# Decay parameters and page table: contiguous broadcast rows and on-chip rearrangement in place of element-wise software loads

## The chip, the cores and the metric

The kernel runs on one core of one Trainium2 chip. The time is what the device takes for one execution, in microseconds (us); lower is better. A core has TensorE (PE; PEld is its weight load), VectorE (DVE), ScalarE (ACT), GpSimd (POOL) and SyncE (SP), each with its own instructions in a fixed order, and 16 DMA engines that move data between the chip's main memory and the on-chip memory of 128 partitions. A DMA that SyncE issues goes to the hardware queue q1, one that GpSimd issues to the software queue q0.

## What is computed

One inference step of a single decoder layer, in float32: 256 prompt tokens and 8 x 4 decoding tokens, model width 4096. The change touches the parameters of two of the three mixers, the gates of the delta rule and the paged cache.

```python
m = silu(c) @ w_ada + b_ada                          # modulation: shift, scale, gate
h = rmsnorm(x, g_norm) * (1 + scale) + shift
u_a, v_a, ..., a_b, b_b, q_c, k_c, ... = split(h @ w_in)      # one input projection
# delta rule: 16 heads, per-head decay
g = -exp(dn_a_log) * softplus(a_b + dn_dt_bias)      # dn_a_log, dn_dt_bias: 16 numbers each
beta = sigmoid(b_b)
o_b, s_new = gated_delta(q, k, v, g, beta, s0)
# sparse attention of the decoding tokens: page_table (8, 16) names the pages of the cache
kidx_past = cache_kidx[page_table]
idx = top_k(score(q_idx, kidx_past), 256)
k_sel, v_sel = cache_k[page_table[idx // 128], idx % 128], cache_v[...]
x = x + gate * (concat(y_a, y_b, y_c) @ w_out)
```

## The kernel before

A weaver writes the whole program at build time. Its main stream is a list of units: a `Gemm` unit multiplies one k-tile of 128 rows of w_in or w_out with the 288 tokens, an `Ada` unit makes modulation columns from w_ada. Every float32 weight tile `w` that is loaded (512 KB, two k-tiles, 4 buffers) is split into a high part `wh` by ScalarE and a low part `wl` by VectorE (4 buffers each), and TensorE adds three products into `acc`: wh with hH, wh with hL, wl with hH. The tiles `wa` and `ada` are weights and results of the modulation. Between the steps of this stream the weaver sets stages of side chains (Python generators), at places that it picks with its own rough clocks of the engines; `yield [tile]` goes on when the clock says that the tile is there. The order of each engine's instructions is fixed by this. SyncE issues all weight loads, one after the other, each once a buffer is free.

Phase 1 makes the modulation and runs the first columns of w_in group by group over 11 steps of feature tiles (`STEPS`; `lb` is its list of units by step). Phase 2 is opened by `phase2_open`: it frees the pools of phase 1 and starts the chains `small_gen` (indexer keys, decay, key and value rows), `idx_sample_gen` (indices of the pages, indexer of the decoding tokens), `sample_gen` and `prompt_gen` (attention), beside the rest of w_in; the delta rule, the gated MLP and the output projection follow.

At the third step from the end of phase 1 a chain with two parts is started:

```python
lb[-3][0].pre.append(lambda: W.push(lane(load_pages(), load_decay())))
```

`load_pages` reads the page table by 25 GpSimd loads into three tiles of int32: `ptp` (one entry for each partition), `pt2` (two entries) and `ptv` (eight entries), each in the layout that the index arithmetic of `idx_sample_gen` wants. `load_decay` fills the tiles `nega` (from dn_a_log) and `dtb` (from dn_dt_bias), 128 partitions x 36 columns: columns 0 to 31 hold the 16 heads twice, side by side (head, chunk), the same for all partitions, and columns 32 to 35 hold, for the 32 partitions of each of 4 groups, every fourth head. Each is written by two loads of 128 x 16 numbers whose neighbours lie two columns apart, and four loads of 32 x 4 numbers read four numbers apart. In `small_gen`, `nega` is first used by `A.activation(nega, nega, AF.Exp)`; in `idx_sample_gen`, the page tiles are used by the casts into `ptf` and `ptvf`, and the index tiles `ix8`, `ixk`, `ixv` feed the indirect gathers of `kraw` and `vraw`.

Every instruction goes through one recording helper, so the profile gives line 71 for all; tiles tell them apart.

Of the kernel before, what the change touches and what calls it, by code (L numbers as in the profile page):

```python
# [60 lines left out]
class Eng:  # L61
    """An engine whose instructions are noted by the weaver as they are emitted."""
# [15 lines left out]
class Gen:  # L78
    """A chain of stages that is emitted between the steps of the main stream.

    A stage that yields a function goes on when the function says so; one that yields tiles, when they are there.
    """
# [5 lines left out]
class Weaver:  # L88
    """Emits the main stream (weight loads, splits, matrix products) with the chains in between.

    The instructions are emitted in an order that suits the in-order engines: rough clocks of the engines tell when
    the operands of a chain's next stage are there.
    """
# [13 lines left out]
    # ---- clocks  # L107
# [18 lines left out]
    @staticmethod  # L126
    def span(ap):
        """The part of a tile that is used: the first to the last free element, and the partitions."""
        row = math.prod(list(ap.tensor.shape)[1:])
        dims = [(st, n) for st, n in ap.ap if n > 1]  # L130
        lo, p, n = ap.offset % row, ap.offset // row, 1
        if dims and dims[0][0] == row:
            n = dims.pop(0)[1]
        hi = lo + 1 + sum((k - 1) * abs(st) for st, k in dims)
        return (lo, hi, p, p + n) if hi <= row else (0, 1 << 40, 0, 1 << 40)

    def tile(self, pool, shape, dt, tag, name, bufs):
        """A tile; it can be written when its place's last tile is not used any more."""
# [68 lines left out]
    # ---- chains  # L207
# [37 lines left out]
    def finish(self, gens, until=None):  # L245
        """Emits the rest of the given chains, and of others where they wait for them."""
# [16 lines left out]
    def slot(self, name, n):  # L263
        """A chain goes on here when fewer than n others hold the named slot."""
# [4 lines left out]
    def lane(self, n=1):  # L269
        """A chain goes on here when its next n DMAs can start at once: each waits for the 8th before it."""  # L270
        yield lambda: all(self.lanes[(self.n_dma + i) % 8] <= self.t["T"] + 0.5 for i in range(n))

    def calm(self):
        """A chain goes on here with a large DMA when the weight loads leave the DMA queues some room."""
# [9 lines left out]
    def bank(self, n=1):  # L284
        """A chain goes on here when n banks are free."""
# [16 lines left out]
    # ---- main stream  # L302
    def prefetch(self, cur):
        """Loads and splits for the units after cur, as far as the buffers go."""
# [70 lines left out]
def tile_hybrid_step(ctx: ExitStack, tc: tile.TileContext, I, O):  # L375
# [39 lines left out]
    # ---------------------------------------------------------------- constants  # L415
# [4 lines left out]
    # 9 columns per k-tile; a quadrant takes 32, whose other rows go unused  # L420
# [15 lines left out]
    # ---------------------------------------------------------------- main stream  # L436
# [21 lines left out]
    class Gemm(Unit):  # L458
        """A k-tile of a group of up to 4 column tiles; two k-tiles are loaded together."""
# [38 lines left out]
    def group(w_ap, segs, tiles, kbs, finish, XH=hH, XL=hL):  # L498
# [5 lines left out]
        # the last two k-tiles go together, so that the tiles end one by one  # L504
# [5 lines left out]
    class Ada(Unit):  # L510
        """Modulation columns: the quadrants of the array take a quarter of a k-tile's columns each,

        or, of two k-tiles, half the columns of one each.
        """
# [46 lines left out]
    def ada_fin1(st, k0, n):  # L561
        """Shift and scale of n feature tiles, then their modulated tokens."""
# [40 lines left out]
    # ---------------------------------------------------------------- pools and loads of the first phase  # L603
# [14 lines left out]
    # the normed tokens lie where the low parts of the modulated ones go  # L618
# [8 lines left out]
    def load_x(i):  # L627
        src, n, _ = xsrc[i]
        if i == 2:
            # a quarter of a row on a partition  # L630
# [25 lines left out]

    ptp, pt2, ptv = (const([P, n], f"pt{n}", I32) for n in (1, 2, NB))
    pt = I["page_table"]

    def load_pages():  # L660
        G.dma_start(ptp, pt.rearrange("b (j o) -> (b j) o", o=1))
        for b in range(4):
            for u in range(2):
                p0 = 32 * b + 16 * u
                G.dma_start(pt2[p0:p0 + 16], bass.AP(tensor=pt.tensor, offset=pt.offset + 16 * b, ap=[[1, 16], [64, 2]]))
            yield from W.pause(4)
        for j in range(16):
            G.dma_start(ptv[8 * j:8 * j + 8], bass.AP(tensor=pt.tensor, offset=pt.offset + j, ap=[[0, 8], [16, NB]]))
            yield from W.pause(2)
# [129 lines left out]
    # ---------------------------------------------------------------- phase 1: modulation and the first columns  # L799
    def y_copy(f):  # L800
        """Frees the place of the low parts while half a tile's tokens are still to be modulated."""
# [96 lines left out]
    # the modulation of a step's feature tiles runs ahead of the products with them  # L898
# [13 lines left out]
    # spread so that the loads are as even as the steps allow  # L912
# [16 lines left out]
    # ---------------------------------------------------------------- phase 2  # L929
# [41 lines left out]
    def load_decay():  # L971
        for t, src in ((sc_["nega"], I["dn_a_log"]), (sc_["dtb"], I["dn_dt_bias"])):
            tpv = t[:, 0:32].rearrange("p (h c) -> p h c", c=2)
            for c in range(2):
                G.dma_start(tpv[:, :, c], bass.AP(tensor=src.tensor, offset=src.offset, ap=[[0, P], [1, 16]]))
            for hl in range(4):
                G.dma_start(t[32 * hl:32 * hl + 32, 32:36],
                            bass.AP(tensor=src.tensor, offset=src.offset + hl, ap=[[0, 32], [4, 4]]))
                yield from W.pause(2)

    def small_gen():
        sm = VT["c", 0]
        X.ki2 = tl("pa", [P, NTOK], "ki2")
# [23 lines left out]
        for t, o in ((av, 80), (bv, 96)):  # L1007
            tpv = t[:, 0:32].rearrange("p (h c) -> p h c", c=2)
            for c in range(2):
                V.tensor_copy(tpv[:, :, c], smt[:, c, o:o + 16])  # L1010
        yield [abD]
        for t, o in ((av, 80), (bv, 96)):
            dma2(t[:, 32:36], abD[0 if o == 80 else 1].rearrange("(g l) t -> (l t) g", l=4))
        # key and value rows, token-major
# [72 lines left out]
    # ---------------------------------------------------------------- attention  # L1087
# [99 lines left out]
    def idx_sample_gen():  # L1187
        # gather indices: 16-row pieces of the indexer pages, 4-row pieces of the key and value pages
# [6 lines left out]
        # 16 where the second half of the partition's 32 is  # L1195
# [13 lines left out]
        yield [ptp, pt2, ptv]  # L1209
        V.tensor_reduce(sub16, sv, axis=AX.X, op=OP.max)  # L1210
        ptf = tl("ap", [P, 3], "ptf")
        V.tensor_copy(ptf[:, 0:1], ptp)
        V.tensor_copy(ptf[:, 1:3], pt2)
# [6 lines left out]
        # row (page, eighth of the page, step) of the value pages, for partition (page, eighth)  # L1220
        ptvf = tl("ap", [P, NB], "ptvf")
        V.tensor_copy(ptvf, ptv)
# [45 lines left out]
        # scores: partition (quarter of the pages, token), column (page of the quarter, key of the page)  # L1268
# [78 lines left out]
    def topk_gen():  # L1347
        """The 256 best keys of every token: the best of the 4 segments in order, the lists merged, ties by position."""
        SC = X.SC
        # sums over the segments of a token, and over the segments before  # L1350
# [3 lines left out]
        for a in range(2):  # L1354
            for dq in range(-3, 4) if a == 0 else range(-3, 0):
                # partition p = 32 q' + r' counts for column 32 q + r where q' = q + dq and r' = r
# [1102 lines left out]
```

## Time and profile before

| | |
|---|---|
| three runs | 2720.19, 2716.18, 2720.14 us; median 2720.14 |
| the profiled execution: span from first to last instruction | 2716.4 us (no other time of this execution is recorded) |
| TensorE busy | 2553.7 us, 94% of the span |
| VectorE, ScalarE, GpSimd busy | 1622.0 (60%), 1062.6 (39%), 511.4 us (19%) |
| DMA | 616.09 MB, 227 GB/s in the mean |

Busy shares are means over stages with different limits. A stage is read by which wait ends last in it; the time of an engine that waits for nothing in a stage and is always busy is that stage's bound.

### The profile page before, as it was taken

What the parts mean: (1) busy time and instruction counts of PE and PEld (TensorE: products, weight loads), DVE (VectorE), ACT (ScalarE), POOL (GpSimd) and SP (SyncE); (2) the same over time, 40 slices, a digit from 0 to 9 for tenths busy, and PEclk for the clock granted to TensorE, in tenths of its full rate; (3) what the DMA queues carried; (4) which work ended last, traced back from release to release, by engine and by line L of the source; (5) the groups of instructions that cost most, each with busy time, mean ns of one, the idle gap of its engine ahead of it and who ended that gap; (6) DMA issues with size and microseconds to landing.
All of it is one profiled execution on the core that took longest, in us unless ns stands there. A gap on an engine that the chain in (4) does not pass through costs nothing.

```text
span 2716.4 us, 55357 instructions
## 1 busy us (share of the span) xinstructions
PE 2553.7 (94%) x21190; PEld 2275.1 (84%) x21190; DVE 1622.0 (60%) x3595; ACT 1062.6 (39%) x2440; POOL 511.4 (19%) x1169
## 2 busy tenths in 40 slices
PE   6999999992699999999999999999999999999997
PEld 3788888882579788878889988989989999999997
DVE  3477655551357778854457567667666567555554
ACT  4433222220224544334344444444444444444443
POOL 2000000201000123054453333442431210000000
PEclk9999999996799999999999999999999999999998
DMA  9999998898865657677777576567567466455554
GB/s 293 346 323 333 333 308 304 289 318 41 202 224 179 187 192 263 224 247 255 263 233 226 177 229 213 185 202 256 172 209 252 155 185 213 157 185 175 176 182 167
DMA packets 376849, 616.09 MB, mean 227 GB/s; under 512 B 49784, under 2 KB 150252, under 8 KB 376584
## 3 DMA queue, kind: packets, MB, share of 16 engines
q1 hardware_dynamic: 364296, 574.58, 64.3%
q0 software_dynamic: 12288, 37.97, 6.6%
q8 instruction: 167, 2.74, 0.4%
q14 instruction: 98, 0.80, 0.1%
HBM read 587.50 MB, written 24.95 MB: 225 GB/s over the span
## 4 chain that ended last, share of the span: by engine, by line
PE 83%; DMA 6%; another core or an unknown queue 3%; DVE 3%; issue 2%; POOL 2%; ACT 1%; SPq 0%; ACTq 0%; POOLq 0%; DVEq 0%
PE acc L71 65%; PE ada L71 7%; DMA w<-in_w_in_dram 2%; DMA wa<-in_w_ada_dram 1%; DMA vraw<-in_cache_v_dram,ixv 1%; PE Sup L71 1%; PE kT L71 1%; DVE wl L71 1%; PE YP L71 1%; PE v L71 1%; POOL vraw L71 1%; PE gram L71 1%; PE o L71 1%; PE S L71 1%
## 5 line engine op out<-in xcount | busy, mean ns | idle before, releaser
L71 DVE TENSOR_TENSOR wl<-w,wh 128x512 fp32r<-128x512 f32 (+1 forms) x1216 | 807.2, 682 | 810.0 <-ACT wh L71 783.4
L71 PE MATMUL acc<-hH,wh 128*128 128x288 f32 (+1 forms) x3744 | 1179.6, 315 | 58.8 <-ACT wh L71 47.6
L71 ACT CAST wh<-w 128x512 fp32r<-128x512 f32 (+1 forms) x1216 | 717.8, 611 | 1307.7 <-PE acc L71 916.4
L71 PE MATMUL acc<-hL,wh 128*128 128x288 f32 (+1 forms) x3744 | 1108.6, 296 | 0.4 <-DVE hL L71 0.4
L71 PE MATMUL acc<-hH,wl 128*128 128x288 f32 (+1 forms) x3744 | 1107.0, 296 | 0.4 <-DVE wl L71 0.4
L71 PEld LDWEIGHTS acc<-hH,wh 128*128 128x128 f32 (+1 forms) x3744 | 706.7, 189 | 201.2 <-ACT wh L71 92.6
L71 PEld LDWEIGHTS acc<-hL,wh 128*128 128x128 f32 (+1 forms) x3744 | 708.3, 189 | 7.9 <-issue 6.7
L71 PEld LDWEIGHTS acc<-hH,wl 128*128 128x128 f32 (+1 forms) x3744 | 707.4, 189 | 1.9 <-DVE wl L71 1.9
L71 PE MATMUL acc<-mL,wh 128*128 128x288 f32 x1024 | 302.7, 296 | 3.3 <-DVE mL L71 3.3
L71 PE MATMUL acc<-mH,wh 128*128 128x288 f32 x1024 | 304.4, 297 | 0.0
L71 PE MATMUL acc<-mH,wl 128*128 128x288 f32 x1024 | 302.9, 296 | 0.0
L71 PE MATMUL ada<-wa,cT 128*32 128x256 f32 x2048 | 159.2, 395 | 46.0 <-DMA wa<-in_w_ada_dram 44.9
L71 PEld LDWEIGHTS acc<-mL,wh 128*128 128x128 f32 x1024 | 193.1, 189 | 3.6 <-DVE mL L71 3.6
L71 PEld LDWEIGHTS acc<-mH,wl 128*128 128x128 f32 x1024 | 193.2, 189 | 0.0
L71 PEld LDWEIGHTS acc<-mH,wh 128*128 128x128 f32 x1024 | 193.0, 188 | 0.2
L71 PEld LDWEIGHTS ada<-wa,cT 128*32 128x32 f32 x2048 | 50.4, 110 | 97.0 <-DMA wa<-in_w_ada_dram 45.9
L71 DVE TENSOR_TENSOR zb<-zb,acc 128x288 f32<-128x288 f32 x160 | 70.6, 452 | 45.4 <-PE acc L71 44.4
L71 POOL TENSOR_TENSOR htmp<-yT,gaT 128x32 f32<-128x32 f32 x20 | 7.7, 386 | 474.6 <-DVE gaT L71 474.6
L71 POOL TENSOR_SCALAR frs<-frs 128x1 f32<-128x1 f32 (+1 forms) x3 | 0.9, 297 | 453.5 <-DVE frs L71 453.4
L71 PE MATMUL ada<-w,cT 128*32 128x256 f32 x1024 | 82.2, 391 | 0.0
L71 DVE TENSOR_TENSOR R<-R,R 128x248 f32<-128x248 f32 (+30 forms) x248 | 72.4, 292 | 6.9 <-DMA R<-dD 0.6
L71 POOL TENSOR_SCALAR tap<-xp,cwT 128x32 f32<-128x32 f32 x144 | 74.2, 515 | 0.4
(452 smaller groups left out, 2401.1 us busy)
## 6 DMA issues: line engine op xcount, KB each, us to landing
w<-in_w_in_dram SPq DMA_DIRECT2D x464, 512.0 KB
wa<-in_w_ada_dram SPq DMA_DIRECT2D x160, 512.0 KB
w<-in_w_ada_dram SPq DMA_DIRECT2D x128, 512.0 KB
w<-in_w_out_dram SPq DMA_DIRECT2D x128, 512.0 KB
wa<-in_w_ada_dram SPq DMA_DIRECT2D x192, 256.0 KB
St<-in_state_dn_dram SPq DMA_DIRECT2D x16, 512.0 KB
out_dram<-St SPq DMA_DIRECT2D x16, 512.0 KB
X<-in_x_prompt_dram SPq DMA_DIRECT2D x8, 512.0 KB
```

The costliest lines, as they stand in the source:

```text
L71: r = f(*a, **k)
```

## The change

The two parameter vectors are read in `small_gen`, at the opening of phase 2, as one row of 16 numbers (64 bytes) for each of the 128 partitions, by two loads on SyncE into `hp`. Twelve small VectorE copies put them where `nega` and `dtb` want them. The page table is read in `idx_sample_gen` as one row of all 128 entries (512 bytes) for each partition, by one load on SyncE into `pts`; VectorE casts it, multiplies it with masks (`ident`, `ptm`, `ptj`, which GpSimd makes) and sums along the row, so that each partition keeps its own entries. `load_pages`, `load_decay`, their pauses and the line that starts them are gone. The rest of the diff drops comments and is left out here.

```diff
-    ptp, pt2, ptv = (const([P, n], f"pt{n}", I32) for n in (1, 2, NB))
-    def load_pages():
-        G.dma_start(ptp, pt.rearrange("b (j o) -> (b j) o", o=1))
-        for b in range(4):
-            for u in range(2):
-                p0 = 32 * b + 16 * u
-                G.dma_start(pt2[p0:p0 + 16], bass.AP(tensor=pt.tensor, offset=pt.offset + 16 * b, ap=[[1, 16], [64, 2]]))
-            yield from W.pause(4)
-        for j in range(16):
-            G.dma_start(ptv[8 * j:8 * j + 8], bass.AP(tensor=pt.tensor, offset=pt.offset + j, ap=[[0, 8], [16, NB]]))
-            yield from W.pause(2)
...
-    def load_decay():
-        for t, src in ((sc_["nega"], I["dn_a_log"]), (sc_["dtb"], I["dn_dt_bias"])):
-            tpv = t[:, 0:32].rearrange("p (h c) -> p h c", c=2)
-            for c in range(2):
-                G.dma_start(tpv[:, :, c], bass.AP(tensor=src.tensor, offset=src.offset, ap=[[0, P], [1, 16]]))
-            for hl in range(4):
-                G.dma_start(t[32 * hl:32 * hl + 32, 32:36],
-                            bass.AP(tensor=src.tensor, offset=src.offset + hl, ap=[[0, 32], [4, 4]]))
-                yield from W.pause(2)
-
     def small_gen():
         sm = VT["c", 0]
+        hp = tl("pa", [P, 2, 16], "hp")
+        for i, src in enumerate((I["dn_a_log"], I["dn_dt_bias"])):
+            dma(hp[:, i], bass.AP(tensor=src.tensor, offset=src.offset, ap=[[0, P], [1, 16]]))
...
+        yield [hp]
+        for i, t in enumerate((nega, dtb)):
+            tpv = t[:, 0:32].rearrange("p (h c) -> p h c", c=2)
+            for c in range(2):
+                V.tensor_copy(tpv[:, :, c], hp[:, i])
+            for hl in range(4):
+                q = slice(32 * hl, 32 * hl + 32)
+                V.tensor_copy(t[q, 32:36], hp[q, i].rearrange("p (g l) -> p l g", l=4)[:, hl])
         yield [abD]
...
     def idx_sample_gen():
+        pts = tl("ap", [P, SEG], "pts", 1, tag="M")
+        pt = I["page_table"]
+        ptB, ptF, ptT = pts[:, 0:P].bitcast(I32), pts[:, P:2 * P], pts[:, 2 * P:3 * P]
+        dma(ptB, bass.AP(tensor=pt.tensor, offset=pt.offset, ap=[[0, P], [1, P]]))
...
-        yield [ptp, pt2, ptv]
+        ptm = pts[:, 384:448].rearrange("p (b j) -> p b j", j=16)
+        G.memset(ptm, 0.0)
+        for u in range(2):
+            G.affine_select(ptm, ptm, pattern=[[-32, 4], [-1, 16]], compare_op=OP.not_equal, fill=1.0,
+                            base=-16 * u, channel_multiplier=1)
+        ptj = pts[:, 448:464]
+        G.affine_select(ptj, ones[:, 0:16], pattern=[[-8, 16]], compare_op=OP.is_ge, fill=0.0, base=0,
+                        channel_multiplier=1)
+        G.affine_select(ptj, ptj, pattern=[[8, 16]], compare_op=OP.is_ge, fill=0.0, base=7, channel_multiplier=-1)
+        yield [ptB]
         V.tensor_reduce(sub16, sv, axis=AX.X, op=OP.max)
         ptf = tl("ap", [P, 3], "ptf")
-        V.tensor_copy(ptf[:, 0:1], ptp)
-        V.tensor_copy(ptf[:, 1:3], pt2)
+        ptvf = tl("ap", [P, NB], "ptvf")
+        V.tensor_copy(ptF, ptB)
+        V.tensor_tensor(ptT, ptF, ident, op=OP.mult)
+        V.tensor_reduce(ptf[:, 0:1], ptT, axis=AX.X, op=OP.add)
+        V.tensor_tensor(ptT.rearrange("p (h n) -> p h n", h=2), ptF.rearrange("p (h n) -> p h n", h=2),
+                        pts[:, 384:448][:, None].to_broadcast([P, 2, 64]), op=OP.mult)
+        V.tensor_reduce(ptf[:, 1:3], ptT.rearrange("p (h n) -> p h n", h=2), axis=AX.X, op=OP.add)
+        V.tensor_tensor(ptT.rearrange("p (b j) -> p b j", j=16), ptF.rearrange("p (b j) -> p b j", j=16),
+                        ptj[:, None].to_broadcast([P, NB, 16]), op=OP.mult)
+        V.tensor_reduce(ptvf, ptT.rearrange("p (b j) -> p b j", j=16), axis=AX.X, op=OP.add)
...
-        ptvf = tl("ap", [P, NB], "ptvf")
-        V.tensor_copy(ptvf, ptv)
...
-    lb[-3][0].pre.append(lambda: W.push(lane(load_pages(), load_decay())))
```

The instructions move at three places. On GpSimd, in the third step from the end of phase 1, these rows stand between the modulation of the feature tiles (`htmp`), and the 25 page-table loads stand likewise one step of feature tiles earlier; a row gives operation, output and input, the shape of the output side (partitions, then elements), and a count. Before:

```order
L71 TENSOR_TENSOR htmp<-htmp,shT 128x4x8
L71 DMA nega<-in_dn_a_log_dram 128x16x1 x2
L71 DMA nega<-in_dn_a_log_dram 32x4x1 x4
L71 DMA dtb<-in_dn_dt_bias_dram 128x16x1 x2
L71 DMA dtb<-in_dn_dt_bias_dram 32x4x1 x4
L71 TENSOR_TENSOR htmp<-yT_102,gaT 128x4x8
```

Now these rows and those of the page table are gone and the `htmp` rows follow each other; the last dimension of 1 in their shapes is a piece of one number.

On SyncE, at the opening of phase 2, behind the stores of the gate columns (`zD`). Before:

```order
L71 DMA zD_178<-zb_1263 128x288
L71 DMA w<-in_w_in_dram 128x2x512
L71 DMA wiD<-smt 32x16
L71 DMA abD<-v_c_571 32x32
L71 DMA out_dram<-smt 128x64 x2
```

Now:

```order
L71 DMA zD_175<-zb_1260 128x288
L71 DMA hp<-in_dn_a_log_dram 128x16
L71 DMA hp<-in_dn_dt_bias_dram 128x16
L71 DMA pts<-in_page_table_dram 128x128
L71 DMA w<-in_w_in_dram 128x2x512
L71 DMA wiD<-smt 32x16
L71 DMA abD<-v_c_568 32x32
```

The three new loads stand ahead of the first weight load behind the stores; all rows of SyncE ahead of this place are as before.

On VectorE at the same place, behind the index constants (`iop`); `pt` are the page tiles, `smt` and `wq` the transposed small columns, `wl` the splits of the main stream. Before:

```order
L71 TENSOR_SCALAR ptvf<-ptvf,iop 128x8
L71 TENSOR_TENSOR ixv<-ptvf,iof 128x64
L71 COPY smt<-smt 128x224
L71 COPY smt<-smt 32x112
L71 TENSOR_SCALAR wq<-smt 128x32
L71 TENSOR_TENSOR wl<-w,wh 128x512 x3
```

Now:

```order
L71 TENSOR_SCALAR iop<-iop 128x1
L71 COPY smt<-smt 128x224
L71 COPY smt<-smt 32x112
L71 TENSOR_SCALAR wq<-smt 128x32
L71 TENSOR_TENSOR wl<-w,wh 128x512 x2
L71 COPY av<-smt 128x16 x2
L71 COPY bv<-smt 128x16 x2
L71 COPY nega<-hp 128x16 x2
L71 COPY nega<-hp 32x4 x4
L71 COPY dtb<-hp 128x16 x2
L71 COPY dtb<-hp 32x4 x4
```

Before, the index arithmetic (it ends with `ixv`) stood ahead of `smt` and of all these splits. Now two `wl` splits come first, then the copies from `hp`, then the arithmetic on `pts` and the index arithmetic, and behind it the third and fourth split. TensorE's rows are the same up to the opening of phase 2; behind it the same products stand in a slightly other order.

## Rows read from the trace of the kernel before

**Rows 1.** The profile's page: the span, and the span in 40 equal slices of 67.9 us (PE: busy tenths of TensorE; GB/s: what the DMA engines moved).

```profile
span 2716.4 us, 55357 instructions
...
PE   6999999992699999999999999999999999999997
...
GB/s 293 346 323 333 333 308 304 289 318 41 202 224 179 187 192 263 224 247 255 263 233 226 177 229 213 185 202 256 172 209 252 155 185 213 157 185 175 176 182 167
```

**Rows 2.** Busy time by stage, core 0: the stretch in us from the span's start, its length, then busy time and instructions of PE, PEld, DVE, ACT and POOL, the granted clock of TensorE (1.00 is 2.4 GHz), the busy share of the 16 DMA engines, and GB/s.

```profile
560.00:616.00 56.00, 56.00 (x474) 47.24 (x474) 30.87 (x62) 16.59 (x30) 5.39 (x11) 1.00 0.90 315
616.00:720.00 104.00, 26.91 (x208) 22.30 (x207) 13.43 (x28) 6.49 (x14) 6.58 (x10) 0.62 0.83 66
720.00:776.00 56.00, 55.93 (x456) 47.79 (x453) 31.21 (x59) 17.10 (x30) 0.00 (x0) 1.00 0.85 291
```

**Rows 3.** Waits that end between 627 and 706 us: who waited for whom, total us, times, the longest.

```profile
ACT wh L71 <- DMA w<-in_w_in_dram: 84.5, 1, 84.5
...
PE acc L71 <- ACT wh L71: 45.9, 1, 45.9
POOL dtb L71 <- DMA nega<-in_dn_a_log_dram: 38.1, 4, 19.1
```

**Rows 4.** The chain of work that ended last, around the stall: start us, length us, what.

```profile
611.13 0.57 PE ada L71 x8
...
615.09 0.57 PE ada L71 x8
...
620.31 84.45 another core or an unknown queue
```

**Rows 5.** TensorE's instructions in order of time: start us, length us, operation, output and inputs, count, and in brackets the idle time before it and what ended it.

```profile
623.37 0.64 PE L71 MATMUL ada<-wa,cT 128*32 128x256 f32 x8
...
627.10 0.29 PE L71 MATMUL acc<-hH,wl 128*128 128x288 f32 x1
658.57 1.08 PE L71 MATMUL ada<-wa,cT 128*32 128x256 f32 x8 [31.18 <-DMA wa<-in_w_ada_dram]
705.52 0.61 PE L71 MATMUL acc<-hH,wh 128*128 128x288 f32 x1 [45.87 <-ACT wh L71]
...
711.02 1.07 PE L71 MATMUL ada<-wa,cT 128*32 128x256 f32 x16
```

**Rows 6.** DMA between 613.5 and 705.5 us: first queues (packets, MB, share of the 16 engines' time), then issues (output and input, queue, count, KB each, median us from issue to landing).

```profile
q0 software_dynamic: 424, 0.04, 72.5%
q1 hardware_dynamic: 1468, 2.82, 8.9%
...
nega<-in_dn_a_log_dram POOLq DMA_DIRECT2D x2, 8.0 KB, 33.5
dtb<-in_dn_dt_bias_dram POOLq DMA_DIRECT2D x2, 8.0 KB, 73.4
```

**Rows 7.** Busy time in the stretch in which the page-table loads are issued, columns as in rows 2.

```profile
519.40:537.70 18.30, 18.30 (x157) 15.55 (x160) 11.88 (x24) 6.53 (x12) 13.80 (x26) 1.00 0.92 301
```

**Rows 8.** The page-table tiles: the loads into them (least, median and longest time of the issue in ns, first and last start in us), and the time from issue to landing.

```profile
L71 POOL DMA_DIRECT2D pt<-in_page_table_dram x25: 504/561/638, 519.5 to 537.1; - x25
...
DMA to landing us min/median/max: 3.5/5.1/6.6
```

**Rows 9.** SyncE's queue where the second phase opens: start us, length us, issues.

```profile
893.21 2.34 SPq L71 DMA_DIRECT2D zD<-zb  x4
900.40 0.38 SPq L71 DMA_DIRECT2D w<-in_w_in_dram  x1
```

**Rows 10.** VectorE at the same place, columns as in rows 5.

```profile
896.72 0.15 DVE L71 TENSOR_REDUCE sub<-sv 128x1 f32<-128x4 f32 x1
...
898.85 0.55 DVE L71 COPY smt<-smt 128x224 f32<-128x224 f32 x2
...
899.41 1.88 DVE L71 TENSOR_TENSOR wl<-w,wh 128x512 fp32r<-128x512 f32 x3
...
903.56 0.25 DVE L71 COPY av<-smt 128x16 f32<-128x16 f32 x2
...
904.61 0.68 DVE L71 TENSOR_TENSOR wl<-w,wh 128x512 fp32r<-128x512 f32 x1
```

**Rows 11.** Groups of VectorE's instructions between 890 and 910 us, forms apart: output and input, shapes, count, busy us, mean ns of one, idle before.

```profile
L71 DVE SCALAR_TENSOR_TENSOR psc<-prl,wq,psc 128x128 f32<-128x128 f32 x3 | 1.0, 350 | 0.1
```

**Rows 12.** A row reduction on VectorE (tile pst of the attention): least, median and longest ns, first and last start, forms.

```profile
L71 DVE TENSOR_REDUCE pst<-ps x16: 286/354/420, 967.3 to 1018.3; 128x1 f32<-128x128 f32 x8, 128x1 f32<-128x256 f32 x8
```

**Rows 13.** ScalarE, then TensorE, behind the first weight load of the second phase, columns as in rows 5.

```profile
907.67 0.62 ACT L71 CAST wh<-w 128x512 fp32r<-128x512 f32 x1 [2.45 <-DMA w<-in_w_in_dram]
...
908.62 0.69 PE L71 MATMUL kvt<-ident,v_kv 128*128 128x128 f32 x2 [2.64 <-ACT ktok L71]
```

**Rows 14.** Busy time from the opening of the second phase to the end, columns as in rows 2.

```profile
890.00:960.00 70.00, 64.40 (x543) 52.52 (x541) 54.19 (x183) 33.07 (x92) 9.52 (x23) 0.95 0.56 174
960.00:2716.40 1756.40, 1712.18 (x14181) 1575.55 (x14181) 1096.99 (x2429) 760.35 (x1832) 441.10 (x992) 0.99 0.64 208
```

**Rows 15.** Busy time in a stretch of the last phase, columns as in rows 2.

```profile
2380.00:2448.00 68.00, 68.00 (x519) 67.89 (x518) 37.59 (x67) 28.66 (x52) 0.00 (x0) 1.00 0.55 184
```

**Rows 16.** DMA issues between 2312 and 2652 us that read one row of 512 numbers for all 128 partitions.

```profile
gfb<-in_g_final_dram SPq DMA_DIRECT2D x7, 256.0 KB
```

More of the change, by code (lines that the diff above doesn't have):

```diff
@@ L655, in tile_hybrid_step @@
     G.dma_start(onT, I["dn_onorm"].rearrange("o p -> p o"))
-    ptp, pt2, ptv = (const([P, n], f"pt{n}", I32) for n in (1, 2, NB))
-    pt = I["page_table"]
-    def load_pages():
-        G.dma_start(ptp, pt.rearrange("b (j o) -> (b j) o", o=1))
-        for b in range(4):
-            for u in range(2):
-                p0 = 32 * b + 16 * u
-                G.dma_start(pt2[p0:p0 + 16], bass.AP(tensor=pt.tensor, offset=pt.offset + 16 * b, ap=[[1, 16], [64, 2]]))
-            yield from W.pause(4)
-        for j in range(16):
-            G.dma_start(ptv[8 * j:8 * j + 8], bass.AP(tensor=pt.tensor, offset=pt.offset + j, ap=[[0, 8], [16, NB]]))
-            yield from W.pause(2)
     W.take()
```

## The prediction

> **What bounds the kernel now.** The 40 slices of the page come first: TensorE (PE) is at 9 tenths almost everywhere, but at 2 and 6 in the tenth and eleventh slice, and in the tenth slice the DMA engines move 41 GB/s after some 300 in each before [rows 1]. The stages around it say the same: 56.00 us busy of 56.00 ahead of the hole, 26.91 of 104.00 in it, 55.93 of 56.00 behind it [rows 2]. So phase 1 is bound by TensorE on either side, and between them something holds it. The waits name it: ScalarE's split of a weight tile (wh) waits 84.5 us for its load from w_in, and TensorE waits 45.9 us for that split [rows 3]; the chain that ended last has one piece of 84.45 us there, which the profile can put down to no engine [rows 4]. While these loads hang, the DMA engines are not idle: the software queue q0 holds 72.5% of the 16 engines' time with 0.04 MB, the weight loads' queue q1 8.9% [rows 6]. What is issued on q0 there are the twelve loads of the decay parameters; the four large ones land after 33.5 and 73.4 us in the median, and GpSimd's own last issues wait for their landing [rows 3, 6]. I read this as: the one-number pieces of these loads occupy the engines, and the weight loads queue behind them.
>
> **What the stall is worth.** Ahead of it TensorE runs a step of 8 ada products and 24 acc products in 615.09 - 611.13 = 3.96 us [rows 4]. A group of 8 ada products begins at 623.37 and the last acc product of its step at 627.10 [rows 5]. Unhindered, the next 8 ada products would begin at 623.37 + 3.96 = 627.33 and the 16 after them at 631.29. They begin at 658.57 and 711.02 [rows 5]. The stream is late by 711.02 - 631.29 = 79.7 us. That holds the idle time, 31.18 + 45.87 = 77.1 us, and the 24 acc products behind it, which start at 705.52 and take 5.5 us, where 3.4 is usual (3.96 less the ada products): the granted clock is 0.62 in this stage, 1.00 around it [rows 2, 5]. Lower bound of the gain here: the idle time alone, 77.1. Upper bound: 80, since the stages around the hole leave no idle time to win. I take 79.7, because the operations are the same and in the same order on TensorE's and SyncE's rows up to the second phase.
>
> **The page-table loads** go too: 25 issues, 128 + 8x32 + 16x64 = 1,408 pieces. They land after 3.5 to 6.6 us [rows 8], and TensorE is busy 18.30 of 18.30 us meanwhile [rows 7]. Their removal is worth nothing: four loaded weight buffers and four split ones cover them. GpSimd's issue time goes as well and nobody waits for it.
>
> **What is added at the opening of the second phase.** Three loads on SyncE: two of 128 rows of 64 bytes, one of 128 rows of 512 bytes, 384 contiguous pieces. They stand behind four stores, at 0.59 us each 895.6 to 897.3, and the weight load behind them is issued at 900.40 now [rows 9], so the queue has the room. Their price on the engines: nothing below; above, as if each piece cost what a piece of the decay loads costs: 0.725 x 92 us x 16 engines / 9,216 pieces = 0.116 engine-us [rows 6], times 384 / 16 = 2.8 us. I take the low end, since 256 KB loads of one row for all partitions run in the last phase with TensorE at 68.00 of 68.00 us [rows 15, 16], and the loaded weight buffers ahead of TensorE cover either.
>
> VectorE is where it could show. Today 896.72 to 898.85 is the index arithmetic and the next three wl splits stand at 899.41 [rows 10]. After the change two wl come first, at about 896.8 + 0.6 (smt, wq) = 897.4 to 898.7; then av and bv (0.3), twelve copies from hp at 0.09 to 0.17 each (1.0 to 2.0), a cast, three products and three reductions over 128 columns at most 0.35 each (2.1 to 2.5) [rows 11, 12], and the old index arithmetic less its casts (1.6). The third wl ends at 904.3 to 905.9 if hp and the table are there in time; the nearest landing times, 3.5 to 6.6 us [rows 8], put hp at 899.1 to 902.7 and could push it to 908. In the stream before, the third wl ended at 901.3. TensorE has two k-tiles of 12 products ahead of it, which with what is woven in last to about 904. So a new wait of 0.3 to 4 us. Against it stands a wait that loses its cause: TensorE idles 2.64 us because ktok stands behind a split on ScalarE that waits for a weight load [rows 13]; in the new order ktok stands ahead of that split. I take 0 for the sum, -3 to +4.
>
> **The rest of the second phase** holds the same instructions, but the weaver places attention and delta-rule pieces some 10 to 70 products later. TensorE has 1756.40 - 1712.18 = 44.2 us idle from 960 us to the end, the tail of the kernel in it [rows 14]. A re-weave may move a quarter of that either way; I take 0, -10 to +10.
>
> **The sum** for the profiled execution: 2716.4 - 79.7 + 0 + 0 = 2636.7 us. No time of its own beside the span is given for it; the three runs lie at 2716.18 to 2720.19 and their median is 3.7 above the span. On the median's footing: 2720.1 - 79.7 = 2640.4, so 2640.
>
> **Rivals.**
> *Part comes back at the opening (B).* If hp or the table lands late, VectorE stands at the first nega copy with the table work and two wl behind it, and TensorE stands for those; weight loads behind SyncE's three issues slip too. 12 to 35 us lost there, 2652 to 2675. For it: VectorE is 54.19 of 70.00 us busy there [rows 14]. Against: 4 us is the most that the landing rows give.
>
> *The change does not remove the stall, or little of it (C).* The page-table loads are software loads of one-number pieces as well, and 25 of them cost TensorE nothing [rows 7, 8]. Were the twelve decay loads as cheap, the stall would have another owner, and the time would stay at 2720, or 2680 and more if they own part. Against: 9,216 pieces instead of 1,408, all within a few microseconds, and q0's 72.5% [rows 6]. The Trainium skill bears on this in "DMA: Bandwidth & Descriptors", Anatomy of one DMA: about 2.0 us fixed for a software load plus its bytes at 436 GB/s. By that the twelve would need some 24 us one after the other, an estimate from the page, and the return could not be over 24: 2696. The trace disagrees: a load of 8 KB takes 33.5 us and more [rows 6].
>
> *Slower (D).* The new loads still read one place for 128 partitions. If that, per byte, and not the number of pieces is what made the decay loads slow, 36.9 KB in 92 us become 16.4 + 65.5 = 81.9 KB, some 200 us, in front of the first weight load of the second phase; it ends slower once they hold the weights for over 80 us. Against: the 256 KB rows named above.
>
> *More than the stall (E).* The new order also removes idle time behind 960 us: under 2630.
>
> **How the numbers follow.** A, the stall goes and 0 to 10 us either way from the re-weave, 0.82, its own range 2630 to 2652; B 0.09; C 0.03; D 0.02; E 0.04. The range 2630 to 2656 leaves out the larger part of B (0.06), C, D and E, 0.15 together. 0.2% of this kernel, about what a measurement can tell from no change, is 5.4 us: faster 0.96 (A, B, E and a part of C), same 0.02 (the rest of C), slower 0.02 (D).
>
> **What would show it.** Right: the tenth and eleventh slices at 9 tenths of PE and some 300 GB/s; no wait of wh for w over 5 us between 600 and 720; steps of 3.96 us through 627; q0 nearly empty in phase 1; clock 1.00 there; phase 2 opens some 80 us earlier, near 814. The first nega copy on VectorE without more than 4 us of idle time ahead of it. Wrong: a hole of the same length at the same place (C), or a hole at the opening of the second phase with waits of VectorE for in_dn_a_log or in_page_table (B, D).

## The result, and the profile after

| | |
|---|---|
| the changed kernel, first set of runs | 2654.27, 2646.74, 2652.58, 2651.12 us; median 2651.85 |
| the kernel before, same set | 2716.18 to 2721.41 us; median 2720.16 |
| ratio, 95% interval | 0.9745 [0.9732, 0.9759]: faster |
| the profiled execution of the changed kernel | 2654.27 us, span 2652.5 us |
| the same kernel in two later sets of five runs | medians 2641.37 and 2640.40 us, ratios 0.9707 [0.9685, 0.9729] and 0.9710 [0.9685, 0.9735] |

The first set lies 11.9 us over the forecast of 2640, the two later ones 1.4 and 0.4; the forecast range of 2630 to 2656 holds all three medians. The kernel won some 68 us in the first set and 78 in the others.

The page of the changed kernel (span, TensorE's 40 slices of 66.3 us, GB/s; compare [rows 1]):

```profile
span 2652.5 us, 55324 instructions
...
PE   6999999999999999999999999999999999999997
...
GB/s 289 345 320 321 342 315 296 304 312 307 232 153 217 178 238 217 200 283 221 266 233 192 182 242 207 177 241 233 179 195 261 149 202 181 178 182 175 177 186 164
...
q0 software_dynamic: 11040, 37.92, 4.3%
```

The tenth and eleventh slices are at 9 tenths and move 307 and 232 GB/s; the hole is gone. The stage that held it, by the columns of [rows 2]:

```profile
560.00:616.00 56.00, 56.00 (x473) 47.79 (x470) 31.19 (x62) 16.35 (x29) 2.92 (x8) 1.00 0.92 320
616.00:720.00 104.00, 103.93 (x852) 88.51 (x851) 58.47 (x112) 31.95 (x58) 0.00 (x0) 1.00 0.82 273
```

103.93 us busy of 104.00 at clock 1.00, where it was 26.91 at 0.62. TensorE's ada products through this place (columns of [rows 5]):

```profile
625.16 0.64 PE L71 MATMUL ada<-wa,cT 128*32 128x256 f32 x8
629.11 0.64 PE L71 MATMUL ada<-wa,cT 128*32 128x256 f32 x8
633.06 1.07 PE L71 MATMUL ada<-wa,cT 128*32 128x256 f32 x16
```

From the first group of 8 to the 16 there are 633.06 - 625.16 = 7.90 us now, and 711.02 - 623.37 = 87.65 before [rows 5]. The stall was worth 79.75 us at its own place; the prediction took 79.7.

The opening of the second phase. First SyncE's queue, then VectorE, then TensorE (start us, length us, what; in brackets the idle time before it and what ended it; compare [rows 9, 10, 13]):

```profile
815.45 2.06 SPq L71 DMA_DIRECT2D zD<-zb  x4
817.56 0.47 SPq L71 DMA_DIRECT2D hp<-in_dn_a_log_dram  x1
...
820.81 0.38 SPq L71 DMA_DIRECT2D w<-in_w_in_dram  x1
```

```profile
822.45 0.84 DVE L71 COPY nega<-hp 128x16 f32<-128x16 f32 x6 [1.35 <-DMA hp<-in_dn_a_log_dram]
...
824.23 0.22 DVE L71 CAST pts<-pts 128x128 f32<-128x128 int32 x1
...
827.70 1.29 DVE L71 TENSOR_TENSOR wl<-w,wh 128x512 fp32r<-128x512 f32 x2
```

```profile
834.80 0.44 PE L71 MATMUL kvt<-ident,v_kv 128*128 128x128 f32 x2 [0.42 <-ACT ktok L71]
```

The four stores stand at 815.45 instead of 893.21, and the phase opens 77.8 us earlier. VectorE waits 1.35 us for hp and not at all for the page table. The wait behind ktok is 0.42 us instead of 2.64. TensorE's longest wait between 812 and 860 us is a new one, for `wq` (total us, times, longest); for a `wl` it doesn't wait there at all:

```profile
PE pidx L71 <- DVE wq L71: 1.4, 1, 1.4
```

### The profile page after: what moved, and what is told of

It is laid out like the page before. It is cut to its first block, busy times and chain, and to the rows that moved or that the text cites. A ratio compares the mean times of both kernels' runs of the same rounds, so it can differ in the third digit from the quotient of the medians.

```text
span 2652.5 us, 55324 instructions
## 1 busy us (share of the span) xinstructions
PE 2560.9 (97%) x21190; PEld 2279.1 (86%) x21190; DVE 1623.5 (61%) x3611; ACT 1062.0 (40%) x2440; POOL 492.3 (19%) x1137
## 4 chain that ended last, share of the span: by engine, by line
PE 86%; DMA 6%; DVE 2%; issue 2%; POOL 2%; ACT 1%; SPq 0%; another core or an unknown queue 0%; ACTq 0%; POOLq 0%; DVEq 0%
PE acc L71 68%; PE ada L71 7%; DMA wa<-in_w_ada_dram 2%; PE kT L71 1%; PE Sup L71 1%; DMA kraw<-in_cache_k_dram,ixk 1%; DVE wl L71 1%; PE YP L71 1%; DMA w<-in_w_in_dram 1%; PE v L71 1%; PE gram L71 1%; DMA vraw<-in_cache_v_dram,ixv 1%; PE o L71 1%; POOL vraw L71 1%; PE S L71 0%
## 5 line engine op out<-in xcount | busy, mean ns | idle before, releaser
L71 PEld LDWEIGHTS acc<-hH,wh 128*128 128x128 f32 (+1 forms) x3744 | 708.4, 189 | 152.0 <-issue 81.9
L71 PE MATMUL ada<-wa,cT 128*32 128x256 f32 x2048 | 159.2, 395 | 15.8 <-DMA wa<-in_w_ada_dram 14.3
```

Of the source, the lines that this page charges most:

```text
L71: r = f(*a, **k)
```

## The experiments

In kernels 1 to 6, and in the two on neighbouring places, every instruction that the edit doesn't name stands in the order of the kernel before: `W.note` books a load on the weaver's clocks without issuing it, so that nothing else moves. One measure serves the kernels on the loads: TensorE's idle time between 613 and 720 us, the length of that window less the busy time; before the change it is 77.1 us.

**1. Half the pieces.**

```diff
-                G.dma_start(tpv[:, :, c], bass.AP(... [[0, P], [1, 16]]))
+                if c == 0:
+                    G.dma_start(tpv[:, :, c], bass.AP(... [[0, P], [1, 16]]))
...
+            nc.vector.tensor_copy(tpv[:, :, 1], tpv[:, :, 0])
         A.activation(nega, nega, AF.Exp)
```

> The kernel before, with the two second 128x16 loads of the decay parameters (chunk 1 of nega and dtb) replaced by two VectorE copies from chunk 0 just ahead of the first use; every other instruction of every engine stands in the same order. 10 of 12 software loads, 5,120 of 9,216 one-number pieces and 0.56 of the bytes stay. If the pieces (or the bytes) cost, the stall of 79.7 us falls to 0.56 of it, 44 us, and the time to about 2720 - 35 = 2685 (2675 to 2692). If each software load costs the same whatever it holds, 10/12 of the stall stays: 2707. If something else owns the stall: 2720.

**2. The same loads into contiguous rows.**

```diff
-                G.dma_start(tpv[:, :, c], bass.AP(... [[0, P], [1, 16]]))
+                nc.gpsimd.dma_start(hq[2 * i + c], bass.AP(... [[0, P], [1, 16]]))
...
-                G.dma_start(t[32 * hl:32 * hl + 32, 32:36], bass.AP(... + hl, ap=[[0, 32], [4, 4]]))
+                nc.gpsimd.dma_start(hs[i][32 * hl:32 * hl + 32], bass.AP(... + 4 * hl, ap=[[0, 32], [1, 4]]))
```

> The kernel before, with the same twelve software loads at the same place on GpSimd, of the same number of bytes from the same two 64-byte rows for all partitions, but into contiguous rows of scratch tiles (768 pieces of 64 or 16 bytes instead of 9,216 of 4), and twelve VectorE copies from there ahead of the first use; the rest in the same order. If the number of pieces owns the stall: 768 x 0.116 engine-us / 16 = 5.6 us of the engines, hidden, no wait of a split for its weight load over 5 us, time 2640 (2634 to 2650). If the software queue, or reading one place for 128 partitions, owns it, the hole stays whole: 2715 to 2725.

**3. The same pieces on the hardware queue.**

```diff
-                G.dma_start(tpv[:, :, c], bass.AP(... [[0, P], [1, 16]]))
+                nc.sync.dma_start(tpv[:, :, c], bass.AP(... [[0, P], [1, 16]]))
```

> The kernel before, with the same twelve one-number loads issued at the same point of the program by SyncE on the hardware queue instead of by GpSimd on the software queue; the rest in the same order. If the pieces themselves cost, whatever queue carries them, the weight loads stand behind them as before: a hole of 70 to 100 us, time 2710 to 2740. If the software queue is what is slow, the hole is gone: 2636 to 2650.

**4. The same pieces from places of their own.**

```diff
-                G.dma_start(tpv[:, :, c], bass.AP(tensor=src.tensor, ... ap=[[0, P], [1, 16]]))
+                G.dma_start(tpv[:, :, c], bass.AP(tensor=cw4.tensor, ... ap=[[16, P], [1, 16]]))
```

> The kernel before, with the twelve one-number software loads reading 128 (or 32) different rows of dn_conv_w instead of the one row of the decay parameters, same pieces, same destinations (the decay parameters are thereby replaced by other numbers; times only). If the pieces cost: the hole stays, 2715 to 2725. If it is the repeated read of one place that is slow (the mechanism by which the new broadcast loads could have been slow too): the hole shrinks to less than a third, 2640 to 2665.

What the four gave, one row each in their order: the window 613 to 720 us (columns of [rows 2]).

```profile
613.00:720.00 107.00, 65.58 (x528) 54.92 (x528) 36.59 (x73) 20.06 (x38) 9.44 (x18) 0.81 0.82 178
```

```profile
613.00:720.00 107.00, 106.93 (x874) 91.51 (x873) 60.43 (x117) 32.08 (x59) 6.54 (x14) 1.00 0.83 272
```

```profile
613.00:720.00 107.00, 39.43 (x287) 31.43 (x287) 19.46 (x42) 10.15 (x20) 1.29 (x4) 0.67 0.28 83
```

```profile
613.00:720.00 107.00, 106.74 (x868) 90.88 (x868) 60.92 (x118) 32.04 (x58) 10.59 (x16) 1.00 0.87 275
```

| | time, us (one run each; before 2727.51 beside them) | TensorE idle, 613 to 720 |
|---|---|---|
| 1: 5,120 of 9,216 pieces | 2685.11 | 41.4 |
| 2: contiguous rows, same 64 bytes for all | 2640.24 | 0.1 |
| 3: hardware queue | 2711.26 | 67.6 |
| 4: one-number pieces, 8 KB of different numbers | 2640.83 | 0.3 |

The first three came out as the pieces' theory has it: 2685 was forecast and 2685.11 measured (42 us under the run of before beside it, where 35 was forecast), the hole goes with contiguous rows, and it stays (shorter by 9.5 us) on the hardware queue. So it is not the number of loads and not the bytes, and the other queue doesn't cure it. Each time is one run, and the kernel before lay between 2711 and 2728 us over all its runs, so the 87 us that kernels 2 and 4 gained beside 2727.51 don't contradict 80. The fourth contradicts the pieces' theory. The pieces are the same 9,216, of the same size, to the same destinations, and nothing is left of the hole. How long the queue q0 held the 16 engines in the window of [rows 6], 613.5 to 705.5 us, in kernels 1, 2 and 4 (packets, MB, share of the 16 engines' time):

```profile
q0 software_dynamic: 352, 0.02, 35.8%
```

```profile
q0 software_dynamic: 384, 0.04, 2.6%
```

```profile
q0 software_dynamic: 448, 0.04, 3.3%
```

In engine time that is 0.725 x 92 x 16 = 1,067 engine-us before [rows 6], 527 in kernel 1, 38 in kernel 2 and 0.033 x 92 x 16 = 49 in kernel 4. A piece that reads a place of its own costs 49 / 9,216 = 0.005 engine-us, one that reads what all others read 0.116 in the mean. On the software queue both conditions are needed: many short reads, and of the same place. Sixteen short reads of one 64-byte row aren't slow by themselves: in kernel 4 each partition of the large loads makes them, each from 64 bytes of its own.

The mean hides a difference. The kernel before has four large loads (128 x 16 pieces, 2,048 each) and eight small ones (32 x 4, 128 each), and the small ones read the same two rows. Kernel 1 has two large loads less, and 352 packets instead of 448, so a large load makes 48 packets and a small one 32. The queue q0 in the kernel before from 613.5 to 696 us and from 696 to 712, then in kernel 1 from 616 to 658 and from 658 to 674:

```profile
q0 software_dynamic: 314, 0.04, 80.8%
q0 software_dynamic: 134, 0.00, 0.6%
```

```profile
q0 software_dynamic: 215, 0.02, 78.3%
q0 software_dynamic: 137, 0.00, 0.6%
```

The 134 and 137 packets at the end are, by their number and place in the queue, the last four small loads and a few packets more. They hold the engines for 0.006 x 16 x 16 = 1.5 engine-us, 0.003 for each of their 512 pieces. So nearly all the price sits in the large loads: 1,067 / 8,192 = 0.130 engine-us a piece before and 527 / 4,096 = 0.129 in kernel 1, which leaves nothing for the eight small ones that both have. The loads into `dtb` in the kernel before:

```profile
DMA to landing us min/median/max: 48.1/64.9/82.7
```

The longest is that of the last large load, issued at 618.1 us or later. From the first issue at 613.5 to this landing that is 87 us or more, some 10.7 ns for each of the 8,192 reads: the reads of the large loads seem to go one after the other, whichever engine asks. Why the small loads of the same row don't pay isn't tested; they have fewer pieces each, and read every fourth number only.

The Trainium skill, in "DMA: Bandwidth & Descriptors", Rules for kernel authors, says of a last dimension that isn't contiguous that it lowers to one descriptor per element and should be made contiguous. Kernel 4 has one-number pieces too and loses nothing, so here this alone is not the price.

GpSimd's issues in kernel 4:

```profile
614.63 4.61 POOL L71 DMA_DIRECT2D nega<-in_dn_conv_w_dram  x6
619.23 2.88 POOL L71 DMA_DIRECT2D dtb<-in_dn_conv_w_dram  x3
623.91 1.64 POOL L71 DMA_DIRECT2D dtb<-in_dn_conv_w_dram  x3 [1.81 <-DMA nega<-in_dn_conv_w_dram]
```

The twelve loads are issued within 614.63 to 625.55, 10.9 us, and the last 25 of their 448 packets move between 630 and 634 us, 19.4 us behind the first issue at the latest:

```profile
q0 software_dynamic: 25, 0.00, 0.5%
```

The estimate of 24 us for all twelve that the prediction worked out from the Trainium skill ("DMA: Bandwidth & Descriptors", Anatomy of one DMA) is one that such loads keep to; the loads of one place don't.

In kernel 3 the price shows in other rows: SyncE itself hangs in its issues (start us, length us).

```profile
613.12 6.10 SPq L976 DMA_DIRECT2D nega<-in_dn_a_log_dram  x2
619.26 19.22 SPq L980 DMA_DIRECT2D nega<-in_dn_a_log_dram  x1
```

One load of 0.5 KB holds the queue for 19.22 us, and the engines' busy share is 0.28 in this hole, against 0.83 in the hole of the kernel before (616 to 720, [rows 2]). So on this queue the weight loads wait behind SyncE's issuing, and the engines are mostly free. No run reads places of their own on this queue; whether the shared place or the number of pieces is the price here isn't shown.

**How near is the same place?** Two kernels read overlapping rows: partition p starts at number p, and in the second kernel at number 4p (`[4, P]` in the line below).

```diff
-                G.dma_start(tpv[:, :, c], bass.AP(tensor=src.tensor, ... ap=[[0, P], [1, 16]]))
+                G.dma_start(tpv[:, :, c], bass.AP(tensor=cw4.tensor, ... ap=[[1, P], [1, 16]]))
```

> The kernel before, with the twelve one-number software loads reading, for partition p, the 16 numbers from number p on of dn_conv_w (143 neighbouring numbers, 572 bytes, for all partitions) instead of the same 16 for all; same pieces, same destinations, same order (the decay parameters are thereby other numbers; times only). If what is slow is the repeated read of the same few bytes (one 64-byte row): the reads spread over nine such rows, at most a ninth of the hole is left, and the time is 2640 to 2652. If a larger region is what is read one after the other: the hole stays, 2710 to 2728, or a part of it that tells the size.

> As the ninth run, but partition p reads the 16 numbers from number 4p of dn_conv_w on (524 neighbouring numbers, 2.1 KB, each read by up to four partitions; the decay parameters are other numbers; times only). The hole was 80 us with all partitions on 64 bytes, 41 us on 572 bytes and nothing on 8 KB. If it goes by how often the same 64-byte row is read, 2.1 KB are 33 rows and next to nothing is left: 2638 to 2648. If by a region of some 250 to 300 bytes (which would explain the half at 572), about 10 to 12 us of reads are left, mostly hidden: 2638 to 2652. If by a region of 1 KB or more, 30 to 45 us are left: 2668 to 2685.

The same window, 613 to 720 us, of the one and of the other:

```profile
613.00:720.00 107.00, 68.44 (x548) 57.46 (x547) 38.40 (x76) 20.53 (x38) 10.03 (x15) 0.82 0.82 185
```

```profile
613.00:720.00 107.00, 101.86 (x820) 86.41 (x820) 57.00 (x109) 30.71 (x56) 8.00 (x12) 0.98 0.86 259
```

Times were 2680.10 and 2649.16 us (before, beside them: median 2718.6, and 2723.16). The idle time falls from 77.1 us (64 bytes for all) to 38.6 (572 bytes), 5.1 (2.1 KB) and 0.3 (8 KB). The queue q0 in the window of [rows 6], in the one and the other:

```profile
q0 software_dynamic: 448, 0.04, 33.4%
```

```profile
q0 software_dynamic: 448, 0.04, 10.1%
```

That is 492 and 149 engine-us, between the 1,067 of the kernel before and the 49 of kernel 4. "At most a ninth is left" for 572 bytes was wrong: reads collide over more than one 64-byte row. Read as a region whose reads go one after the other, 0.46 of 572 bytes and 0.14 of 2,096 are 264 and 293 bytes, and the 30 to 45 us of a region of 1 KB didn't come. But the partitions that read one number become fewer along with it (128, 16, 4 and 1), and no run separates the two. So the region is a reading; its size, and what part of the memory it belongs to, are open.

**Where the first set's 12 us went.** Against its own sum of 2636.7 us the first profiled execution was 15.8 us long. Kernels 2 and 4, with the second phase in its old order, stood at 2640, so the first theory (W) was that the new order costs it.

**5.** The row loads at the start of the program, the second phase as before:

```diff
+    hp = const([P, 2, 16], "hp")
+    for i, src in enumerate((I["dn_a_log"], I["dn_dt_bias"])):
+        nc.sync.dma_start(hp[:, i], bass.AP(tensor=src.tensor, offset=src.offset, ap=[[0, P], [1, 16]]))
```

> The kernel before, with the decay parameters read as two loads of one 64-byte row for all partitions at the very start of the program (SyncE, behind the loads of x), the twelve VectorE copies behind them, and the page table as before; every other instruction of every engine in the order of the kernel before. Theory W (the changed kernel gets the whole stall back, some 80 us, and gives about 12 back because the pieces of the second phase stand in another order): 2640 (2636 to 2644), 8 to 14 us under the changed kernel on the same chip. Rival (the 12 us were never won: the stall is worth only 68): 2648 to 2655, no faster than the changed kernel.

**6.** The whole change, but its loads, copies and sums are hidden from the weaver (`nc.vector`, `nc.sync` in place of `V`, `dma`), and the old ones booked with `W.note`:

```diff
-        V.tensor_copy(ptf[:, 0:1], ptp)
+        W.note("V", "tensor_copy", (ptf[:, 0:1], ptp), {})
+        nc.vector.tensor_copy(ptF, ptB)
```

> The whole change (three row loads on SyncE at the opening of the second phase, copies, masks, products and sums at the places where their results are wanted), but with the pieces of the second phase woven as in the kernel before: the weaver is told of the old loads and casts and not of the new work. VectorE then meets the page table's load 4 to 5 us early and waits for it, with two or three wl splits behind. Theory W (the order gives the 12 us back): 2638 to 2648. Rival N (the new loads, copies and sums at the opening cost it, whatever the order): 2648 to 2656, as the changed kernel.

**7.** The decay half of the diff alone, run twice; and **8.** the changed kernel, run twice more.

```diff
-    lb[-3][0].pre.append(lambda: W.push(lane(load_pages(), load_decay())))
+    lb[-3][0].pre.append(lambda: W.push(load_pages()))
```

> The decay half of the change alone: row loads and twelve copies at the opening of the second phase as in the changed kernel, the page table by its 25 software loads as before, woven by the weaver's own clocks. Both theories: the stall is gone, so under 2660. If the re-woven order is what gives time back and the page table's part moves most of it (the index arithmetic stands ahead of the splits as before here): 2636 to 2646. If the decay copies give it back: 2648 to 2656.

> The changed kernel once more, on the chip of the other three, for comparison: 2652 (2646 to 2656) if its first runs are typical, and a ratio to the kernel before of 0.9732 to 0.9759.

> The changed kernel a third time. Its nine runs so far lie at 2634 to 2654, and one program's two profiles differ by 18 us. Theory S (it is the spread of the executions, by TensorE's waits and granted clock in the second phase): again some runs under 2642 and some over 2646, median 2638 to 2650. Rival C (each chip has its own level): all runs within 8 us of each other.

> The decay half of the change alone, again, on the chip of the changed kernel's runs. If its lead of 6 us is real: 2633 to 2642 and 4 to 10 us under the changed kernel. If both are one spread: medians within 4 us of each other.

| | median (range), us | ratio to before, 95% interval |
|---|---|---|
| 5, early rows | 2643.55 (2639.78 to 2652.55) | 0.9716 [0.9694, 0.9738] |
| 6, change in old order | 2645.44 (2641.25 to 2648.31) | 0.9724 [0.9708, 0.9740] |
| 7, decay only | 2635.33 (2633.48 to 2638.00) | 0.9686 [0.9667, 0.9705] |
| 8, changed, again | 2641.37 (2634.44 to 2648.21) | 0.9707 [0.9685, 0.9729] |
| changed, third set | 2640.40 (2634.64 to 2646.39) | 0.9710 [0.9685, 0.9735] |
| decay only, beside the third set | 2638.68 (2637.05 to 2645.23) | 0.9711 [0.9687, 0.9734] |

The forecast of 2652 us for the second set missed by 11 us, and with it theory W falls: on one chip the changed kernel is not slower than kernels 5 and 6, which keep the old order. Decay only led by 6.0 us in one set and by 1.7 in the next, with overlapping intervals (the first of the two 0.7 us under the lower of its ranges), so the runs don't show that any version beats the changed one. What they show is a spread: the changed kernel's fourteen runs lie between 2634.44 and 2654.27 us, one program, and each later set alone spans more than the 8 us of rival C (13.8 and 11.8).

Two profiles of that one program, the first (span 2652.5) and that of its second set (2634.4), tell where most of it lies. TensorE's row of the page, first and second:

```profile
PE 2560.9 (97%) x21190; PEld 2279.1 (86%) x21190; DVE 1623.5 (61%) x3611; ACT 1062.0 (40%) x2440; POOL 492.3 (19%) x1137
```

```profile
span 2634.4 us, 55324 instructions
...
PE 2548.9 (97%) x21190; PEld 2270.4 (86%) x21190; DVE 1623.6 (62%) x3611; ACT 1062.6 (40%) x2440; POOL 489.5 (19%) x1137
```

Of the 18.1 us between the spans, 12.0 are busy time of the same 21,190 instructions, and 6.1 idle. Phase 1 has 5.0 of them: the four stores at its end stand at 815.45 in the first and here in the second:

```profile
810.46 2.36 SPq L71 DMA_DIRECT2D zD<-zb  x4
```

The place where most opens up is in the attention, with nearly the same 607 and 609 products (first, then second profile):

```profile
1200.00:1270.00 70.00, 65.76 (x607) 54.99 (x606) 30.92 (x47) 27.25 (x71) 23.79 (x40) 0.95 0.65 215
```

```profile
1191.40:1254.50 63.10, 62.14 (x609) 52.07 (x608) 31.01 (x47) 27.70 (x71) 23.94 (x40) 1.00 0.72 242
```

4.24 us idle against 0.96, and behind it the granted clock at 0.95 against 1.00, so that the products themselves take 3.6 us more. TensorE's waits in these two windows (who waited for whom, total us, times, longest):

```profile
PE Sn L71 <- issue: 2.2, 2, 1.2
PE kT L71 <- DMA kraw<-in_cache_k_dram,ixk: 1.7, 2, 1.0
```

```profile
PE kT L71 <- DMA kraw<-in_cache_k_dram,ixk: 0.8, 2, 0.5
```

Here waits of a microsecond behind gathers and instruction issue come or don't come, and the granted clock is lower in the execution with the longer waits; that the waits lower it isn't tested. Why the first set's four runs all lie at 2646 or more is open. Chance alone is a weak account: the first set's interval lies clear of both later ones, while the kernel before had nearly the same medians beside all three (2720.16, 2719.61 and 2718.60).

## Why the prediction was right, and where it was not

**The stall's place and owner: right.** The decay loads held the weight loads up, and without them TensorE is busy throughout.

**Its size: right.** 79.75 measured at the place, 79.7 taken. Kernel 2, which removes the stall and moves no other instruction on TensorE and SyncE, ran 2638.5 us in its span against the 2636.7 of the sum. One of the signs missed: the eleventh slice moves 232 GB/s, not some 300, with TensorE busy all the same.

**Its reason: half wrong.** "The one-number pieces of these loads occupy the engines" left out what kernel 4 showed: they do so only when they all read the same place. And not all of them did: the eight small loads hardly held the engines. So 9,216 pieces against the page table's 1,408, which was the answer to C, was not the contrast that mattered; the 25 page-table loads have at most 128 pieces each, like the small ones here. That kernel 1 met 2685 to 0.1 us is partly luck: beside its own run of before it gained 42 us, not 35. D, put at 0.02, had a condition that mattered, the same place, but priced it per byte, and 81.9 KB became 200 us. The price of 0.116 engine-us a piece, used for the upper bound of the new loads, is that of short reads of one place and not that of contiguous rows. Kernel 2's contiguous pieces of one place cost 38 / 768 = 0.049, which makes an estimate of 384 x 0.049 / 16 = 1.2 us for the new loads, under the bound of 2.8; hp landed within 4.9 us of its first issue (817.56 to 822.45), as small loads do [rows 8].

**The page-table loads: right**, worth nothing that the runs can tell: kernels 5 and 7 keep them and are as fast.

**The opening of the second phase: right in the sum, by other waits.** Forecast were a new wait of TensorE of 0.3 to 4 us behind the third wl, and against it the end of the 2.64 us behind ktok. The first didn't come: VectorE waited 1.35 us for hp, and TensorE for no wl, but 1.4 us for wq. Of the second 0.42 is left.

**The rest of the second phase, 0 with -10 to +10: the term that was off in the first set.** From the four stores to the end the program took 1823.2 us before, 1837.1 in the first profile after and 1823.9 in that of the second set. So the first profile's 15.8 us over the sum are 13.9 here, the opening included, and 2.0 in phase 1. In the second the phase took 0.7 us more than before, phase 1 was 3.0 us faster than the sum has it, and the span came out 2.3 under it (2634.4 against 2636.7). The term was thought of as a matter of order, and neither this nor kernels 5 and 6 put anything on the new order. What the first set had instead is a slower level of the same program, whose cause stays open. The prediction's 0.2% (5.4 us) for what a measurement can tell was too fine: one program's runs span 19.8 us, 0.75%.

Rivals: B didn't come (VectorE waited 1.35 us for hp, not 12 or more), C, D and E neither.

## What to carry to other kernels

A hole in which the engines move almost nothing while a queue with a few KB holds them is worth looking for: find which loads read the same few bytes many times over in short pieces. Reading the row in one contiguous piece per partition and spreading it on chip cured it here, and reading from places of their own did too; moving the loads to the hardware queue didn't. A gain of some tens of us that sits in one stage could be forecast to a microsecond at its own place, from the step of the stream around it, but a phase with waits of a microsecond spread through it has to be given its spread from several runs, on more than one chip, before a difference of 10 us is explained.

## What the runs showed of the hardware that was not expected

- Short reads of one place, 2,048 to a load on the software queue, seem to go one after the other, at some 10.7 ns each over all 16 engines. Loads of 128 short reads of the same row held the engines for next to nothing, and contiguous rows of it little. Places some hundred bytes apart still collide: idle 77.1, 38.6, 5.1 and 0.3 us for 64 bytes, 572 bytes, 2.1 KB and 8 KB.
- On the hardware queue a load of 0.5 KB, issued behind two such loads of 8 KB, kept SyncE for 19.22 us in its issue, with the engines at 0.28 of their time.
- One program's span differed by 18.1 us between two executions, two thirds of it in busy time; where most opened up, the granted clock was 0.95 against 1.00.
